# Up projections with 512 moving columns, first down projection in tokens, displaced activation slots, and 12 score bursts

## The chip, the cores and the metric

The kernel runs on one core of a Trainium2 chip. The engines of that core that matter are TensorE (PE: matmuls, and PEld: the load of a matmul's stationary operand), VectorE (DVE), ScalarE (ACT), GpSimd (POOL) and SyncE (SP, which issues most transfers). Each engine runs its own instructions strictly in the order in which they stand; semaphores tie the engines together. The metric is the device time of one execution in microseconds, as the median of several runs.

## The reference

A trunk of two layers over one sequence of 256 tokens with 1024 channels, all in float32:

```python
def hybrid_layer(x, ...):
    h = rmsnorm(x, norm_mix)
    proj = h @ w_in          # q, k, v of 24 heads of 64, and three gates of 1024
    ...                      # o_a: 12 dilated-window heads, o_b: 6 block heads, o_c: 6 stick-breaking heads
    merged = gates[:, :, 0] * (o_a @ w_out_a) + gates[:, :, 1] * (o_b @ w_out_b) + gates[:, :, 2] * (o_c @ w_out_c)
    x = x + merged @ w_o
    h = rmsnorm(x, norm_mlp)
    return x + jnp.square(jax.nn.relu(h @ w_up)) @ w_down     # 1024 -> 4096 -> 1024
# two layers, then one rmsnorm
```

The gates pass a sigmoid first. The dilated and block heads use a softmax; the stick-breaking heads use exponentials of sums of log-sigmoids.

## The kernel before

**Numbers.** Every value that TensorE multiplies is kept as two parts, `hi` (rounded to the type fp32r) and `lo` (the rest), and a product is the three matmuls lo·hi, hi·hi and hi·lo, added up in PSUM. ACT writes the `hi`, DVE the `lo`.

**Weights** come in 280 pieces of 128x1024 (`raw`), one transfer each, in the order of use. `split` makes `wh` (L118, ACT) and `wl` (L119, DVE) of a piece, three pieces ahead of TensorE, in 6 buffers each.

**Activations** lie with channels on the partitions: `xres` [128, 8, 256] is the residual. A normalised or scaled copy lies in one of two rotating slots `hl` [128, 2, 8, 256], first all `hi`, then all `lo`, written by `norm_split` (L158 ACT, L159 DVE). A `proj` (L198 to L200) takes one weight piece and 8 channel blocks: 24 matmuls with 256 moving columns.

**A layer, stage by stage.** (1) `v_chunk` (L243 to L245): V in tokens, with 512 moving columns. (2) `qk_pair` and `gate_tile`, in the order MIX_ORDER, and between them the attention units: `a0`, `a1` (six heads each, softmax), `b0` to `b2` (two heads each, softmax), `c0` to `c2` (two heads each, stick-breaking). A unit begins with a burst of score matmuls (`burst`, L283, 64 rows of contraction), then come ACT and DVE work on the scores, transposes (L377 to L379) and the PV matmuls (L310, L311); an `a` unit has two bursts, so that a layer has ten. After the last PV of a pair, `o_head` (ACT L297 `tmp`, DVE L298 `oF`) and `o_split` (ACT L301, DVE L302) write the head pair's channels into the slot `oT`. (3) The sigmoids of the eight gate tiles (L479), held back until after the last exponential, between two loads of the ACT tables (L479 and L482, the second in the first layer alone). (4) The merge: eight times a `proj` over `oT` into a two-bank PSUM tile `s` (two of them rotate), multiplied by the gates on DVE (L495), summed (L496, L497) and split (L498, L499). (5) `w_o`: eight `proj`, each added to `xres` (L507), then `norm_split`. (6) The MLP: `up_pair` makes two `proj` into one PSUM bank, then ACT Relu (L540), ACT Square (L542), DVE CAST (L545) and DVE subtract (L546). The down projection of the first layer, `down` (L557 to L559), has the weights stationary and 256 tokens moving, 768 matmuls; that of the last layer, `down_nat` (L583 to L585), has the activations stationary and 512 weight columns moving, 384 matmuls, with the result in tokens. The down projections of pair i-1 follow the ups of pair i; the last four pieces are kept for the end, where the result is finished part by part. For the first layer that end is: scale by R2 and add to `xres` on DVE (L644, L645), `norm_split`, next layer.

**Order.** The kernel is recorded in program order; a scheduler with priorities (for instance 400 for bursts, 300 for weight splits) then sets the order on each engine. An engine's order is fixed when the kernel is built.

## Time and profile before

| | us |
|---|---|
| median of three runs | 884.33 (883.89 to 885.01) |
| the profiled execution | 884.33 |
| its span, first to last instruction | 882.6 |
| PE busy | 870.9 (99%) |
| DVE busy | 598.9 (68%) |
| ACT busy | 494.2 (56%) |
| POOL busy | 50.7 (6%) |

The span is shorter than the time by 1.7 us that lie around it. The granted TensorE clock is 0.998 of full speed over the span, the higher of its two levels. "Busy" of an engine is the time in which at least one of its instructions was under way; matmuls overlap, so that a record of 0.28 us stands beside the next one 0.12 us later. What a matmul costs in a row of matmuls is therefore read from start to start.

### The profile page before, as it was taken

What the parts mean: (1) busy time and instruction counts of PE and PEld (TensorE: products, weight loads), DVE (VectorE), ACT (ScalarE), POOL (GpSimd) and SP (SyncE); (2) the same over time, 40 slices, a digit from 0 to 9 for tenths busy, and PEclk for the clock granted to TensorE, in tenths of its full rate; (3) what the DMA queues carried; (4) which work ended last, traced back from release to release, by engine and by line L of the source; (5) the groups of instructions that cost most, each with busy time, mean ns of one, the idle gap of its engine ahead of it and who ended that gap; (6) DMA issues with size and microseconds to landing.
All of it is one profiled execution on the core that took longest, in us unless ns stands there. A gap on an engine that the chain in (4) does not pass through costs nothing.

```text
span 882.6 us, 16351 instructions
## 1 busy us (share of the span) xinstructions
PE 870.9 (99%) x6648; PEld 833.1 (94%) x6648; DVE 598.9 (68%) x899; ACT 494.2 (56%) x732; POOL 50.7 (6%) x64
## 2 busy tenths in 40 slices
PE   8999999999999999999999999999999999999996
PEld 7899999999999999999988999999999999999995
DVE  6977878855886554555678878787567865555553
ACT  7756566758365444444466664666573554444442
POOL 3000101000030000000020101010000300000000
PEclk9999999999999999999999999999999999999999
DMA  9755443454556666666565554344554666666641
GB/s 316 258 173 159 144 143 121 155 160 151 180 181 186 187 187 181 180 188 184 151 196 187 174 162 142 122 141 146 168 167 145 214 192 191 189 190 187 189 127 48
DMA packets 43562, 151.47 MB, mean 172 GB/s; under 512 B 4960, under 2 KB 6368, under 8 KB 43488
## 3 DMA queue, kind: packets, MB, share of 16 engines
q1 hardware_dynamic: 43056, 149.90, 55.2%
q8 instruction: 52, 0.85, 0.4%
q10 hardware_dynamic: 432, 0.54, 0.2%
q14 instruction: 22, 0.18, 0.1%
HBM read 149.37 MB, written 1.05 MB: 170 GB/s over the span
## 4 chain that ended last, share of the span: by engine, by line
PE 94%; DVE 2%; DMA 1%; issue 1%; ACT 1%; SPq 0%; POOLq 0%; ACTq 0%
PE mm L198 18%; PE mm L199 18%; PE mm L200 18%; PE s L557 4%; PE s L559 4%; PE s L558 3%; PE s L583 3%; PE s L584 3%; PE s L585 3%; PE s L283 2%; PE s L198 2%; PE s L199 2%; PE s L200 2%; PE s L243 2%; PE s L245 2%; PE s L244 2%
## 5 line engine op out<-in xcount | busy, mean ns | idle before, releaser
L119 DVE TENSOR_TENSOR wl<-raw,wh 128x1024 fp32r<-128x1024 f32 (+1 forms) x282 | 343.8, 1222 | 221.7 <-ACT wh L118 221.1
L118 ACT ACTIVATE wh<-raw 128x1024 fp32r<-128x1024 f32 (+1 forms) x282 | 295.0, 1051 | 274.0 <-PE mm L200 151.1
L198 PE MATMUL mm<-hl,wl 128*128 128x256 f32 x1344 | 382.1, 285 | 1.9 <-DVE xres L507 1.9
L199 PE MATMUL mm<-hl,wh 128*128 128x256 f32 x1344 | 381.3, 284 | 0.0
L200 PE MATMUL mm<-hl,wh 128*128 128x256 f32 x1344 | 379.8, 284 | 0.0
L198 PEld LDWEIGHTS mm<-hl,wl 128*128 128x128 f32 x1344 | 257.3, 191 | 3.7 <-DVE xres L507 2.4
L199 PEld LDWEIGHTS mm<-hl,wh 128*128 128x128 f32 x1344 | 257.3, 192 | 0.9
L200 PEld LDWEIGHTS mm<-hl,wh 128*128 128x128 f32 x1344 | 256.7, 191 | 0.3 <-DVE hl L159 0.2
L557 PE MATMUL s<-ga,wl 128*128 128x256 f32 x256 | 72.6, 284 | 0.0
L558 PE MATMUL s<-ga,wh 128*128 128x256 f32 x256 | 72.4, 283 | 0.0
L559 PE MATMUL s<-ga,wh 128*128 128x256 f32 x256 | 72.2, 283 | 0.0
L169 POOL TENSOR_TENSOR acc<-acc,sq 128x256 f32<-128x256 f32 x28 | 26.9, 962 | 417.4 <-ACT sq L168 242.6
L583 PE MATMUL s<-wl,ga 128*128 128x512 f32 x128 | 50.1, 392 | 0.0
L584 PE MATMUL s<-wh,ga 128*128 128x512 f32 x128 | 50.0, 391 | 0.0
L557 PEld LDWEIGHTS s<-ga,wl 128*128 128x128 f32 x256 | 49.1, 192 | 0.4 <-DVE sq L644 0.2
L585 PE MATMUL s<-wh,ga 128*128 128x512 f32 x128 | 49.5, 389 | 0.0
L558 PEld LDWEIGHTS s<-ga,wh 128*128 128x128 f32 x256 | 49.1, 192 | 0.1
L559 PEld LDWEIGHTS s<-ga,wh 128*128 128x128 f32 x256 | 49.0, 192 | 0.2 <-DVE ga L546 0.2
L198 PE MATMUL s<-hl,wl 128*128 128x256 f32 x128 | 36.5, 285 | 0.0
L199 PE MATMUL s<-hl,wh 128*128 128x256 f32 x128 | 36.2, 283 | 0.0
L200 PE MATMUL s<-hl,wh 128*128 128x256 f32 x128 | 36.2, 283 | 0.0
L410 POOL TENSOR_SCALAR_AFFINE_SELECT wk<-wk 128x256 f32<-128x256 f32 x24 | 18.4, 790 | 221.2 <-DVE wk L422 152.2
(132 smaller groups left out, 1124.4 us busy)
## 6 DMA issues: line engine op xcount, KB each, us to landing
raw<-in_w_dram SPq DMA_DIRECT2D x278, 512.0 KB, 4.2
raw<-in_w_dram SPq DMA_DIRECT2D x4, 256.0 KB, 3.5
xres<-in_x_dram SPq DMA_DIRECT2D x8, 128.0 KB, 5.6
wk<-in_gfin_dram SPq DMA_DIRECT2D x2, 256.0 KB, 4.4
out_dram<-V SPq DMA_DIRECT2D x2, 256.0 KB, 2.3
out_dram<-V ACTq DMA_DIRECT2D x2, 256.0 KB, 2.1
c_maskA<-in_maskA_dram SPq DMA_DIRECT2D x1, 384.0 KB, 6.1
c_rope<-in_rope_dram SPq DMA_DIRECT2D x1, 256.0 KB, 5.7
```

The source lines that it names most:

```text
L118: act.activation(hi[:, c:c + step], r[:, c:c + step], AF.Copy)
L119: dve.tensor_tensor(lo[:, c:c + step], r[:, c:c + step], hi[:, c:c + step].bitcast(F32), op=ALU.subtract)
L169: pool.tensor_tensor(acc, acc, sq, op=ALU.add)
L198: pe.matmul(dst, lo[:, c:c + P], hl[:, 0, koff + k], start=a, stop=False, skip_group_check=True)
L199: pe.matmul(dst, hi[:, c:c + P], hl[:, 0, koff + k], start=False, stop=False, skip_group_check=True)
L200: pe.matmul(dst, hi[:, c:c + P], hl[:, 1, koff + k], start=False, stop=z, skip_group_check=True)
L557: pe.matmul(dst, lo[:, c], uh[:, j % 2], start=a, stop=False, skip_group_check=True)
L558: pe.matmul(dst, hi[:, c], uh[:, j % 2], start=False, stop=False, skip_group_check=True)
L559: pe.matmul(dst, hi[:, c], ul[:, j % 2], start=False, stop=z, skip_group_check=True)
L583: pe.matmul(dst, uh[:, j % 2, k], lo[:, c], start=j == 0, stop=False)
L584: pe.matmul(dst, uh[:, j % 2, k], hi[:, c], start=False, stop=False)
L585: pe.matmul(dst, ul[:, j % 2, k], hi[:, c], start=False, stop=j == 2 * npairs - 1)
```

## The change

**Wide up runs.** A new `proj_wide` takes a weight piece and moves `hi` and `lo` of a channel block as one run of 512 columns: 8 matmuls with `wh` stationary into the two halves of a bank, and 8 with `wl` stationary and 256 columns into the first half; 16 where 24 were. For that, `hi` and `lo` of a block lie side by side: the slots are [128, 8, 2, 256]. Each piece has a PSUM bank of its own. DVE adds the halves (`tensor_reduce`, over a strided view of the bank), for a pair of pieces DVE makes max(t,0)·t, ACT copies it into `uh`, DVE subtracts `ul`.

**First down in tokens.** Both layers use `down_nat`. At the end of the first layer's MLP each of four groups (128 tokens x 512 channels) is scaled on ACT, turned back by four transposes on PE, and added to `xres` on DVE; after the second token half of a channel half come four `norm_split`. The broadcast of R2 goes.

**Displaced slots.** The rotating slots `hl` become two fixed ones, `hl0` and `hl1`, and small unused tiles between `hl0`, `hl1`, `ga` and `wh` move the addresses of what follows them.

**Bursts of two units.** `together` sends the score matmuls of two units as one burst: per layer c0 with the first of a0, then the second of a0, c1 with the first of a1, the second of a1, c2 with b0, b1 with b2. Six per layer. A burst waits until all reads of the previous burst's banks that its units returned (a softmax's minimum pass, a `c` unit's last exponential) are done.

The diff, cut to its core (where only the index order of a slot changes, and where a unit only returns its jobs instead of sending them, lines are left out):

```diff
+
+
+    for tag, shape, bufs, dt in (("hl0", [P, KT, 2, S], 1, F32R),
+                                 ("skip0", [P, 24], 1, F32),
+                                 ("hl1", [P, KT, 2, S], 1, F32R),
+                                 ("skip1", [P, 56], 1, F32),
+                                 ("ga", [P, 3, S], KT, F32),
+                                 ("skip2", [P, 48], 1, F32),
+                                 ("wh", [P, 1024], W_BUFS, F32R), ("wl", [P, 1024], W_BUFS, F32R), ("V", [P, 2, 8, 2, DH], 3, F32R)):
+        T(tag, shape, bufs, dt)
...
-    def hilo_slot():
-        return T("hl", [P, 2, KT, S], 2, F32R)
+    def hilo_slot(i):
+        return T("hl%d" % i, [P, KT, 2, S], 1, F32R)
...
+    def proj_wide(n, hl, bank):
+
+        hi, lo = split(n)
+        for k in range(KT):
+            pe.matmul(bank, hi[:, k * P:k * P + P], hl[:, k].rearrange("p a b -> p (a b)"), start=k == 0, stop=False,
+                      skip_group_check=True)
+        for k in range(KT):
+            pe.matmul(bank[:, 0:S], lo[:, k * P:k * P + P], hl[:, k, 0], start=False, stop=k == KT - 1,
+                      skip_group_check=True)
 
     acc = T("acc", [P, S], 1)
-    hl = hilo_slot()
+    hl = hilo_slot(0)
     for d in range(KT):
         norm_split(hl, 0, d)
         sumsq(d, acc)
...
                 act.activation(t[:, 1], p3[:, 1], AF.Copy)
             QK[f] = t
 
-        def burst(jobs, after=None):
-
+        open_banks = []
+
+        def together(*units):
+
+            made = [u() for u in units]
             before = None
             with tc.high_priority(offset=BPRI):
-                for dst, f, j, qs, ks, flipped, first in jobs:
+                for dst, f, j, qs, ks, flipped, first in sum([m[0] for m in made], []):
                     t, own = QK[f], slice(j * DH, j * DH + DH)
                     q, k = t[own, 0, qs], t[own, 1, ks]
                     i = pe.matmul(dst, k if flipped else q, q if flipped else k, start=first, stop=True, skip_group_check=True)
-                    if before is None and after is not None:
-                        tc.add_manual_dep(i.ins, after.ins.name, READ, reason="the banks are free together")
-                    if before is not None:
+                    if before is None:
+                        for r in open_banks:
+                            tc.add_manual_dep(i.ins, r.ins.name, READ, reason="the banks are free together")
+                    else:
                         tc.add_manual_dep(i.ins, before.ins.name, QUEUED, reason="one burst of scores")
                     before = i
-
-        oT = hilo_slot()
+            open_banks.clear()
+            for m in made:
+                open_banks.append(m[1]())
+
+        oT = hilo_slot(0)
         last_exp = [None]
         T0, T1, TT = slice(0, P), slice(P, S), slice(0, S)
 
...
@@ -466,12 +503,19 @@
             {"v": v_chunk, "qk": qk_pair, "g": gate_tile}[kind](i, n)
             n += MIX_LEN[kind]
             group, u = ATT_AFTER.get((kind, i), (None, 0))
-            if group == "a":
-                att_softmax(QK_A[u], u, units)
+            if group == "c":
+                held.append(att_c(u))
+            elif group == "a" or (group == "b" and (held or u == 1)):
+                sc, va = att_softmax(QK_A[u], u) if group == "a" else att_softmax([QK_B[u]], 2 + u)
+                if group == "b" and not held:
+                    held.append((sc, va))
+                else:
+                    hs, hv = held.pop(0)
+                    units.append(lambda a=sc[0], b=hs[0]: together(a, b))
+                    units += [lambda a=a: together(a) for a in sc[1:]] + hv + va
             elif group == "b":
-                att_softmax([QK_B[u]], 2 + u, units)
-            elif group == "c":
-                att_c(u, units)
+                sc, va = att_softmax([QK_B[u]], 2 + u)
+                units += [lambda a=sc[0]: together(a)] + va
             run_units(UNIT_RATE[kind])
         run_units(len(units))
         with tc.issue_after(last_exp[0].ins):
...
-        if layer < DEPTH - 1:
-            R2 = T("tmp", [P, S], 2)
-            act.activation(R2, bcast(rcol), AF.Square)
 
...
         def up_pair(i):
-            p = mm_bank()
-            proj(p[:, 0:S], npc["u", 2 * i], hl)
-            proj(p[:, S:2 * S], npc["u", 2 * i + 1], hl)
-            s1 = T("wk", [P, 512], WK)
-            act.activation(s1, p, AF.Relu)
-            u = T("wk", [P, 512], WK)
-            act.activation(u, s1, AF.Square)
+            t = T("wk", [P, 2, S], WK)
+            for a in range(2):
+                p = mm_bank()
+                proj_wide(npc["u", 2 * i + a], hl, p)
+                dve.tensor_reduce(t[:, a], p.rearrange("p (a b) -> p b a", a=2), axis=mybir.AxisListType.X, op=ALU.add)
+            u = T("wk", [P, 2, S], WK)
+            dve.scalar_tensor_tensor(u, t, 0.0, t, op0=ALU.max, op1=ALU.mult)
             uh = T("ga", [P, 2, S], KT, F32R)
             ul = T("ga", [P, 2, S], KT, F32R)
-            dve.tensor_copy(uh.rearrange("p a b -> p (a b)"), u)
-            dve.tensor_tensor(ul.rearrange("p a b -> p (a b)"), u, uh.rearrange("p a b -> p (a b)").bitcast(F32), op=ALU.subtract)
+            act.activation(uh, u, AF.Copy)
+            dve.tensor_tensor(ul, u, uh.bitcast(F32), op=ALU.subtract)
             us[i] = (uh, ul)
-
-
-        def down(j, d):
...
-            r2 = T("rc", [P, 2], 8)
-            dve.tensor_tensor(r2, rcol, rcol, op=ALU.mult)
+        r2 = T("rc", [P, 2], 8)
+        dve.tensor_tensor(r2, rcol, rcol, op=ALU.mult)
 
         def down_nat(j, t, h):
             hi, lo = split(npc["d", j])
...
-        groups = [(t, h) for t in range(2) for h in range(2)] if last else [(d,) for d in range(KT)]
-        one = down_nat if last else down
+        groups = [(t, h) for t in range(2) for h in range(2)] if last else [(t, h) for h in range(2) for t in range(2)]
+        one = down_nat
         body = 2 * npairs - TAIL
         for i in range(npairs + 1):
             if i < npairs:
@@ -629,22 +655,27 @@
             finish(1)
             continue
         acc = T("acc", [P, S], 1)
-        hl = hilo_slot()
-        for d in range(KT):
-            if d == 0:
-                for e in range(SKEW):
-                    for j in range(body, 2 * npairs - 2):
-                        down(j, e)
-            if d + SKEW < KT:
+        hl = hilo_slot(0)
+        for i, (t, h) in enumerate(groups):
+            if i == 0:
                 for j in range(body, 2 * npairs - 2):
-                    down(j, d + SKEW)
+                    one(j, t, h)
+            if i + 1 < len(groups):
+                for j in range(body, 2 * npairs - 2):
+                    one(j, *groups[i + 1])
             for j in range(2 * npairs - 2, 2 * npairs):
-                down(j, d)
-            tmp = T("sq", [P, S], 3)
-            dve.tensor_tensor(tmp, down_dst(d), R2, op=ALU.mult)
-            dve.tensor_tensor(xres[:, d], xres[:, d], tmp, op=ALU.add)
-            norm_split(hl, 2 * layer + 2, d)
-            sumsq(d, acc)
+                one(j, t, h)
+            y = T("wk", [P, 512], WK)
+            act.activation(y, acc2[h][:, t], AF.Copy, scale=r2[:, t:t + 1])
+            tb = t_bank()
+            for d in range(4):
+                pe.transpose(tb[:, d * P:(d + 1) * P], y[:, d * P:(d + 1) * P], ident)
+            x4 = xres[:, 4 * h:4 * h + 4, t * P:(t + 1) * P]
+            dve.tensor_tensor(x4, x4, tb.rearrange("p (a b) -> p a b", a=4), op=ALU.add)
+            if t == 1:
+                for d in range(4 * h, 4 * h + 4):
+                    norm_split(hl, 2 * layer + 2, d)
```

What the change does to the order of instructions is shown at three places; all names are tiles with their numbers.

**The end of the attention of the first layer, PE.** `t_432` is the PSUM tile of the last head's PV, `s_460` the first tile of the merge, `mm_448` and `mm_455` the last gate tile's, `hl_23` is `oT`. Before, the last PV and the first of the merge:

```order
L311 MATMUL t_432_2403<-pl_435_2409,V_87_454 64x256
L310 MATMUL t_432_2403<-ph_434_2408,V_87_454 128x128
L311 MATMUL t_432_2403<-pl_435_2409,V_87_454 64x128
L198 MATMUL s_460_2619<-hl_23_169,wl_451_2519 128x256
L199 MATMUL s_460_2619<-hl_23_169,wh_450_2518 128x256
L200 MATMUL s_460_2619<-hl_23_169,wh_450_2518 128x256
```

Seven rows of `s_460` stand there, then 72 of the gates, and then the merge goes on:

```order
L198 MATMUL mm_455_2577<-hl_22_168,wl_447_2487 128x256
L199 MATMUL mm_455_2577<-hl_22_168,wh_446_2486 128x256
L200 MATMUL mm_455_2577<-hl_22_168,wh_446_2486 128x256
L199 MATMUL s_460_2619<-hl_23_169,wh_450_2518 128x256
L200 MATMUL s_460_2619<-hl_23_169,wh_450_2518 128x256
L198 MATMUL s_460_2619<-hl_23_169,wl_451_2519 128x256
```

Now (`t_441` is the last PV's tile, `s_469` and `s_474` the first two of the merge, `hl0_32` is `oT`):

```order
L336 MATMUL t_441_2412<-ph_443_2417,V_96_463 128x256
L337 MATMUL t_441_2412<-pl_444_2418,V_96_463 64x256
L336 MATMUL t_441_2412<-ph_443_2417,V_96_463 128x128
L337 MATMUL t_441_2412<-pl_444_2418,V_96_463 64x128
L207 MATMUL s_469_2628<-hl0_32_178,wl_460_2528 128x256
L208 MATMUL s_469_2628<-hl0_32_178,wh_459_2527 128x256
L207 MATMUL s_474_2665<-hl0_32_178,wl_463_2558 128x256
L208 MATMUL s_474_2665<-hl0_32_178,wh_462_2557 128x256
L209 MATMUL s_469_2628<-hl0_32_178,wh_459_2527 128x256
```

The gate matmuls now all stand ahead of the last PV, and so do 12 of the 24 matmuls of `s_469` and 12 of `s_474`; the next row reads the channel block that the last head pair fills.

**The same place, ACT.** Before (sigmoids of `ga`, weight splits `wh`):

```order
L297 ACTIVATE tmp_436_2416<-t_432_2403 64x256
L301 ACTIVATE hl_23_169<-oF_356_1990 128x256
L479 ACT_TABLE_LOAD
L479 ACTIVATE ga_24_170<-ga_24_170 128x768
L479 ACTIVATE ga_25_171<-ga_25_171 128x768
L479 ACTIVATE ga_26_172<-ga_26_172 128x768
L479 ACTIVATE ga_27_173<-ga_27_173 128x768
L479 ACTIVATE ga_28_174<-ga_28_174 128x768
L479 ACTIVATE ga_29_175<-ga_29_175 128x768
L479 ACTIVATE ga_30_176<-ga_30_176 128x768
L118 ACTIVATE wh_462_2622<-raw_461_2620 128x1024
L118 ACTIVATE wh_467_2659<-raw_466_2657 128x1024
```

Now:

```order
L327 ACTIVATE hl0_32_178<-oF_365_1999 128x256
L523 ACT_TABLE_LOAD
L523 ACTIVATE ga_33_179<-ga_33_179 128x768
L523 ACTIVATE ga_34_180<-ga_34_180 128x768
L523 ACTIVATE ga_35_181<-ga_35_181 128x768
L523 ACTIVATE ga_36_182<-ga_36_182 128x768
L523 ACTIVATE ga_37_183<-ga_37_183 128x768
L523 ACTIVATE ga_38_184<-ga_38_184 128x768
L523 ACTIVATE ga_39_185<-ga_39_185 128x768
L523 ACTIVATE ga_40_186<-ga_40_186 128x768
L526 ACT_TABLE_LOAD
L127 ACTIVATE wh_486_2742<-raw_485_2740 128x1024
```

All eight sigmoids and both table loads stand together, ahead of the first weight split. On DVE that split's other half, `wl_487`, stands ahead of the gate products (L539) from the fourth merge tile on:

```order
L539 TENSOR_TENSOR wk_483_2733<-s_479_2702,ga_35_181 128x768
L128 TENSOR_TENSOR wl_487_2743<-raw_485_2740,wh_486_2742 128x1024
L540 TENSOR_TENSOR wk_483_2733<-wk_483_2733 128x256
L128 TENSOR_TENSOR wl_492_2780<-raw_490_2777,wh_491_2779 128x1024
L543 TENSOR_TENSOR hl1_468_2627<-wk_473_2659,hl1_468_2627 128x256
L543 TENSOR_TENSOR hl1_468_2627<-wk_478_2696,hl1_468_2627 128x256
L541 TENSOR_TENSOR wk_483_2733<-wk_483_2733 128x256
L539 TENSOR_TENSOR wk_488_2770<-s_484_2739,ga_36_182 128x768
```

Ahead of the first of these rows stand the gate products of `s_469` and `s_474`, with their sums.

**From `w_o` into the MLP, PE, first layer.** `mm_536` and `mm_545` are the last tile of `w_o`, `mm_549` and `mm_557` the first of the ups. Before:

```order
L199 MATMUL mm_536_3174<-hl_459_2618,wh_523_3066 128x256
L200 MATMUL mm_536_3174<-hl_459_2618,wh_523_3066 128x256
L198 MATMUL mm_549_3227<-hl_501_2916,wl_529_3104 128x256
L199 MATMUL mm_549_3227<-hl_501_2916,wh_528_3103 128x256
L200 MATMUL mm_549_3227<-hl_501_2916,wh_528_3103 128x256
```

20 rows of `mm_549` and 20 of the next piece stand there ahead of the first that reads the seventh channel block. Now:

```order
L209 MATMUL mm_545_3183<-hl1_468_2627,wh_532_3075 128x256
L215 MATMUL mm_557_3232<-hl0_510_2925,wh_537_3112 128x512 x6
L215 MATMUL mm_561_3256<-hl0_510_2925,wh_542_3149 128x512 x6
L215 MATMUL mm_557_3232<-hl0_510_2925,wh_537_3112 128x512
L215 MATMUL mm_561_3256<-hl0_510_2925,wh_542_3149 128x512
L184 MATMUL t_550_3220<-ones_75,acc_509_2924 128x1 x2
L215 MATMUL mm_557_3232<-hl0_510_2925,wh_537_3112 128x512
L218 MATMUL mm_557_3232<-hl0_510_2925,wl_538_3113 128x256 x8
```

Twelve wide matmuls stand ahead of the first that reads the seventh block.

## Rows read from the trace of the kernel before

**Rows 1.** The page: busy time by engine; the chain that ended last, by engine.

```profile
PE 870.9 (99%) x6648; PEld 833.1 (94%) x6648; DVE 598.9 (68%) x899; ACT 494.2 (56%) x732; POOL 50.7 (6%) x64
...
PE 94%; DVE 2%; DMA 1%; issue 1%; ACT 1%; SPq 0%; POOLq 0%; ACTq 0%
```

**Rows 2.** The waits of PE, grouped: total us, times, longest us.

```profile
PE mm L198 <- DVE xres L507: 1.9, 2, 1.1
```

**Rows 3.** First attention, two stretches of MLP: us; busy PE, PEld, DVE, ACT, POOL.

```profile
53.42:202.00 148.58, 148.58 (x1260) 145.26 (x1261) 115.41 (x216) 91.77 (x157) 9.21 (x12) 1.00 0.49 150
264.00:430.00 166.00, 166.00 (x1384) 165.95 (x1384) 87.17 (x91) 79.27 (x90) 0.71 (x1) 1.00 0.63 185
719.07:831.27 112.20, 112.20 (x721) 102.62 (x721) 60.50 (x61) 54.12 (x62) 0.00 (x0) 1.00 0.64 192
```

**Rows 4.** Timeline of PE in the last layer's MLP: start us, duration us, instruction.

```profile
752.33 0.40 PE L583 MATMUL s<-wl,ga 128*128 128x512 f32 x1
...
754.85 0.39 PE L585 MATMUL s<-wh,ga 128*128 128x512 f32 x1
```

**Rows 5.** Timeline of PE around the first score burst.

```profile
53.02 0.28 PE L199 MATMUL mm<-hl,wh 128*128 128x256 f32 x1
53.14 0.28 PE L200 MATMUL mm<-hl,wh 128*128 128x256 f32 x1
53.35 0.93 PE L283 MATMUL s<-qk 64*128 64x256 f32 x8
54.20 0.39 PE L198 MATMUL mm<-hl,wl 128*128 128x256 f32 x1
54.42 0.28 PE L199 MATMUL mm<-hl,wh 128*128 128x256 f32 x1
```

**Rows 6.** Groups by line and shape: count, busy us, mean ns, idle before.

```profile
L119 DVE TENSOR_TENSOR wl<-raw,wh 128x1024 fp32r<-128x1024 f32 x278 | 340.7, 1229 | 216.4 <-ACT wh L118 215.9
L118 ACT ACTIVATE wh<-raw 128x1024 fp32r<-128x1024 f32 x278 | 292.6, 1057 | 272.4 <-PE mm L200 151.1 <-PE s L559 38.9 <-PE s L585 33.7
L557 PE MATMUL s<-ga,wl 128*128 128x256 f32 x256 | 72.6, 284 | 0.0
...
L546 DVE TENSOR_TENSOR ga<-wk,ga 128x512 fp32r<-128x512 f32 x32 | 22.2, 693 | 1.1
...
L495 DVE TENSOR_TENSOR wk<-s,ga 128x768 f32<-128x768 f32 x16 | 15.2, 952 | 1.3 <-PE s L200 1.3
L283 PE MATMUL s<-qk 64*128 64x256 f32 x96 | 14.7, 411 | 0.0
...
L268 DVE TENSOR_TENSOR qk<-mm,c_rope 128x512 f32<-128x512 f32 x18 | 12.1, 673 | 0.0
...
L283 PE MATMUL s<-qk 64*128 64x128 f32 x96 | 8.4, 280 | 0.0
```

**Rows 7.** The chain that ended last: start us, us, what it was.

```profile
245.24 0.51 DVE xres L507 x2
...
259.90 0.34 DVE xres L507
...
268.07 0.43 PE t L188 x2
...
702.48 0.44 PE t L572 x4
```

**Rows 8.** Timeline of ACT at the end of the first layer's attention.

```profile
202.56 0.38 ACT L297 ACTIVATE tmp<-t 64x256 f32<-64x256 f32 x1
204.00 0.42 ACT L301 ACTIVATE hl<-oF 128x256 fp32r<-128x256 f32 x1 [1.06 <-DVE oF L298]
204.44 1.28 ACT L479 ACT_TABLE_LOAD   x1
205.73 5.25 ACT L479 ACTIVATE ga<-ga 128x768 f32<-128x768 f32 x7
```

**Rows 9.** Timeline of PE at the same place: first gate row after the PV, first merge row after the gates.

```profile
202.12 0.28 PE L198 MATMUL mm<-hl,wl 128*128 128x256 f32 x1
...
210.76 0.28 PE L199 MATMUL s<-hl,wh 128*128 128x256 f32 x1
```

**Rows 10.** Timeline of DVE at the same place.

```profile
203.55 0.42 DVE L298 TENSOR_TENSOR oF<-t,tmp 64x256 f32<-64x256 f32 x1
...
211.96 2.36 DVE L119 TENSOR_TENSOR wl<-raw,wh 128x1024 fp32r<-128x1024 f32 x2 [7.08 <-ACT wh L118]
```

More of the change, by code (lines that the diff above doesn't have):

```diff
@@ L389, in values, with att_c @@
                     o_split(oF, kt_out)
-            units += [score] + [softmax_second] * (G == 3) + [lambda: values(0), lambda: values(1)]
-        def att_c(i, units):
+            return ([softmax_first, softmax_second] if G == 3 else [softmax_one]), [lambda: values(0), lambda: values(1)]
+        def att_c(i):
             f = QK_C[i]
@@ L414, in logs @@
                 st = s_bank()
-                burst([(st[:, j, 0:S], f, j, TT, T0, True, True) for j in range(2)]
-                      + [(st[:, j, S:384], f, j, T1, T1, True, False) for j in range(2)])
-                z = st[:, :, 0:384]
-                ab = T("wk", [P, 2, 384], WK)
-                act.activation(ab, z, AF.Abs)
-                act.activation(ab, ab, AF.Exp, scale=-1.0)
-                act.activation(ab, ab, AF.Ln, bias=1.0)
-                dve.scalar_tensor_tensor(ab, z, 0.0, ab, op0=ALU.max, op1=ALU.add)
@@ L423, in logs @@
-                strict(ab)
-                h, l = hl2(ab)
-                for j in range(2):
-                    for x in (h, l):
-                        pe.matmul(st[:, j, 0:384], negtri, x[:, j], start=False, stop=False, skip_group_check=True)
-                    for n, x in enumerate((h, l)):
-                        pe.matmul(st[:, j, P:S], negones, x[:, j, S:384], start=False, stop=n == 1, skip_group_check=True)
-                a = T("wk", [P, 2, 384], WK)
-                last_exp[0] = act.activation(a, z, AF.Exp)
@@ L432, in logs, with rest @@
-                strict(a)
-                env["a"] = hl2(a)
+                def rest():
+                    z = st[:, :, 0:384]
+                    ab = T("wk", [P, 2, 384], WK)
+                    act.activation(ab, z, AF.Abs)
+                    act.activation(ab, ab, AF.Exp, scale=-1.0)
+                    act.activation(ab, ab, AF.Ln, bias=1.0)
+                    dve.scalar_tensor_tensor(ab, z, 0.0, ab, op0=ALU.max, op1=ALU.add)
+                    strict(ab)
+                    h, l = hl2(ab)
+                    for j in range(2):
+                        for x in (h, l):
+                            pe.matmul(st[:, j, 0:384], negtri, x[:, j], start=False, stop=False, skip_group_check=True)
+                        for n, x in enumerate((h, l)):
+                            pe.matmul(st[:, j, P:S], negones, x[:, j, S:384], start=False, stop=n == 1, skip_group_check=True)
+                    a = T("wk", [P, 2, 384], WK)
+                    last_exp[0] = act.activation(a, z, AF.Exp)
+                    strict(a)
+                    env["a"] = hl2(a)
+                    return last_exp[0]
@@ L435, in values @@
+                return ([(st[:, j, 0:S], f, j, TT, T0, True, True) for j in range(2)]
+                        + [(st[:, j, S:384], f, j, T1, T1, True, False) for j in range(2)]), rest
             def values():
@@ L457, in trunk @@
         units = []
+        held = []
         def run_units(k):
```

99 lines of the change are left out of this document (45 added, 54 removed).

## The prediction

> **What bounds the kernel now.** I read the page first: PE is busy for 99% of the span, and the chain that ended last runs through PE for 94% of it [rows 1]. The grouped waits name only one repeated wait of PE, 1.9 us in two places [rows 2]. So the time is the PE stream plus a few stalls, and the change can act in two ways: it makes the stream shorter, or it makes PE wait where it did not. The second is the one to search for, because ACT and DVE hardly ever make PE wait now. The profiled execution took 884.33 us, which is also the median; 1.7 us of it lie around the span.
>
> **Price of a matmul.** Not the 284 ns of a record [rows 6], since records overlap, but start to start. In the first layer's MLP, 1384 matmuls of 256 columns took 166.00 us: 119.9 ns each [rows 3]. In the last layer ten iterations took 112.20 us and hold 480 such matmuls and 240 of 512 columns: (112.20 - 480 x 0.1199)/240 = 227.7 ns, the switches between the two forms included [rows 3]; inside a run, 11 spacings from 752.33 to 754.85, 2.52 us, give 229 ns [rows 4]. Doubling the columns thus adds 107.8 ns, and 12.1 ns of each matmul do not depend on columns.
>
> This is where a page speaks against the change: the Trainium skill, "TensorE: Matmul & The Clock Gate", section "Wait — 56ns, not 53.3ns?", gives a matmul N/2.4 ns plus about 2.5 ns. By it fewer, wider matmuls would hardly help: the two PE terms below would be about 1.3 and 1.0 us and not 6.3 and 4.7. The trace disagrees for this data type, with 12.1 ns, and decides.
>
> **The change part by part: what PE saves.**
> - Wide ups. A piece costs 24 x 119.9 = 2.878 us now and 8 x 227.7 + 8 x 119.9 = 2.781 after; 64 pieces: 6.2 us.
> - First down in tokens: 768 x 119.9 ns = 92.1 us against 384 x 227.7 = 87.4: 4.7 us.
> - Bursts. Around a burst the spacing before its first matmul is 0.21 instead of 0.12, the one after it 0.22 instead of 0.12: 0.19 us of switching at the edges [rows 5]. The eight matmuls themselves take 0.85 us, against 0.37 if the two row halves ran fully side by side (768 columns at 2.4 GHz and four times 12 ns), so up to 0.48 may be switching as well. I take 0.38 per burst, between 0.19 and 0.67. Twenty bursts (192 score matmuls [rows 6]) become twelve: 8 x 0.38 = 3.0 us, bounds 1.5 and 5.4.
> - The R2 broadcast goes: half of the pair that took 0.43 us in the chain [rows 7], 0.2 us. Sixteen fp32 transposes come: four of the same kind took 0.44 us [rows 7], so 1.8 us, and 0.2 for getting into and out of that type.
> Sum: 6.2 + 4.7 + 3.0 + 0.2 - 2.0 = 12.1 us shorter, bounds 9 and 14.5.
>
> **What PE will wait for.** The order of the changed kernel shows three places.
>
> (1) The end of the attention, both layers. Now 72 gate matmuls, 8.64 us from 202.12 to 210.76 [rows 9], lie between the last PV and the first merge matmul that needs the last heads. They hide the chain tmp 0.38, oF 0.42, hl 0.42, a table load of 1.28 and most of the sigmoids, 0.75 each [rows 8, 10]. In the changed order no gate matmul is left there; the next row of PE reads the last heads' channels. With time zero where `hl` is written: PE waits 1.5 us before it (0.38 + 0.42 + 0.42 and three handovers of about 0.1). Sigmoid 0 ends at 1.28 + 0.75 = 2.1, its product (0.95, L495 [rows 6]) at 3.1, where PE, 24 matmuls on, wants the bank at 2.9: 0.2. Then eight sigmoids end at 7.3 and the second table load at 8.6; `wh` takes 1.06, `wl` 1.2 [rows 6], so wl_487 ends at 10.9. Behind it on DVE stand 0.4 of sum, wl_492 (until about 12.4), three short passes, and only then the product that frees the bank of the fifth merge tile: about 14.4. PE wants that bank at 11.9: 2.5 us. First layer: 1.5 + 0.2 + 2.5 = 4.2. The last layer has no second table load; by the same steps the fifth tile's bank comes at 10.9 against 8.9 wanted, and the next weights 0.3 late: 1.5 + 0.2 + 2.3 = 4.0. Queued behind the late DVE passes are the `hl1` splits and the `w_o` weight splits, which PE needs only later. Together 8.2 us; I take off 0.5 for the chain's step through DVE at 245.24 [rows 7], which a later start will swallow: 7.7. Bounds: 3 (the head chain and half of the rest) and 10.
>
> (2) From `w_o` into the MLP, both layers. PE has 40 matmuls of 256 (4.8 us) as cover there now and still waits 1.9 us in all, for the chain of xres, hl and weight splits on DVE, whose last step is the 0.34 at 259.90 [rows 2, 7]. Twelve wide matmuls are 2.7 us of cover. 2.1 us less cover, of which the faster rest of the run takes up part, since the wide pieces' `wl` half needs no further `lo`: 0.75 more per layer, 1.5. Bounds 0 and 4.
>
> (3) The turn from layer one to two: each transposed group waits for its ACT copy (about 0.6) right behind its own last matmuls. Four such waits, partly filled with V matmuls: 1.5 against 0.7 to 1.1 of stalls now: 0.8. Bounds 0 and 2.5.
>
> Sum of new waits: 7.7 + 1.5 + 0.8 = 10.0 us.
>
> Costed at nothing. The evictions in the MLP: a strided reduce has no row; the nearest are a plain 512 pass from PSUM at 0.67 and one at 0.69 [rows 6]. Per iteration of about 11 us DVE then has four `wl` of 1.2, two reduces and two passes, some 7.5 us; the cover is PE's 11 us, and it would fail only with reduces of over 2.4 us. Of PSUM the Trainium skill ("Advanced Engine Details and Errata", section "Memory Cachelines") says that every two consecutive elements should be contiguous; no run here shows that yet, and it alone would not reach PE. ACT loses two passes per pair and gains one. The displaced slots: matmuls of now show no spacing other than 119.9 over 1384 of them [rows 3]; I take zero, with 3 ns per matmul either way as a bound for the some 2700 that read `hl1`, 8 us. The wait of a burst for the previous one's reads: behind it PE's whole queue stands still, and who waits for that is every projection; my steps through the first burst (c0 with a0) give 10.0 us of ACT, DVE and POOL work until its next PE step against 10.3 us of PE work there, so nothing, but narrowly.
>
> **Sum.** 884.33 - 12.1 + 10.0 = 882.2 us. The gain is nearly given back.
>
> **The rivals.**
> - *The cover holds.* If ACT and DVE are less late at the end of the attention (PE itself being later there, by the chains before it), only the head chain of 1.5 us per layer stays, and with (2) and (3): 884.3 - 12.1 + 5.3 = 877.5. For it: PE in the trace nearly never waits for ACT and DVE. Against it: the order is fixed, and no gate matmul is left to fill. Displaced slots that save 3 ns would land lower still, at 870 to 875. Together 0.24.
> - *Longer attention chains, slower.* A c unit's scores now share burst, ACT and DVE with an a unit's. Decisive point: the 10.3 us of PE work up to the first triangle matmul of a c unit; each further microsecond of chain is a stall, six times in the kernel. With 1.2 us more each: 882.2 + 7.2 = 889.4; with half of it 886. For it: the margin of 0.3 us, and ACT and DVE are busy for 62% and 78% of the attention [rows 3]. Against it: PE now passes ten bursts per layer with no wait at all. Chance 0.26.
> - *Even.* Switching saves only the edges (1.5 in place of 3.0) and the new waits are as reckoned: 883.7; or new waits of 12 us: 884.2. Chance 0.16 beyond what the forecast's own spread holds.
> - *The change does not do what it says:* if a 512 wide run that is half `hi`, half `lo` cost more than the 227.7 of the last layer's downs, the ups would save nothing: 888. Nothing in the trace speaks for it; counted with the slower case.
>
> **How the numbers follow.** The forecast, 880 to 884.4 with 882.2 in the middle, has 0.34, of which some 0.26 lies below 882.56, which is 0.2% under the time of now (a measurement of this kernel can tell about that much from no change). Faster: 0.24 + 0.26 = 0.50. Within 0.2% (882.6 to 886.1): 0.08 of the forecast and 0.16 of the even case: 0.24. Slower: 0.26. The range leaves out 0.1 at each end: low end 873.0, where the rival of the held cover and a little of the slots lie, high end 889.0, nearly the full price of the longer chains. The forecast's own range is 880 to 884.4.
>
> **What would show it.** Right: in the MLP of both layers an iteration step of about 11.0 us in the chain (11.52 and 11.22 now); spacings of 0.12 and 0.227 in the ups; a PE stall of about 1.5 us right after the last PV and one of about 2 us at the fifth merge tile, released by DVE, in both layers; twelve bursts. Wrong: no PE wait at the merge (then the first rival), PE waits at L427's successor or at the bursts of 1 us or more (then the second), an up piece of over 2.85 us (then the last), or spacings of 256 columns that differ from 119.9 ns between the slots.

## The result and the profile after

The changed kernel takes 890.95 us (890.35 to 892.57) against 884.52 us of the kernel before: a ratio of 1.0076, 95% interval 1.0059 to 1.0093. It is slower, and lies outside the forecast range of 873.0 to 889.0. The profiled execution has a span of 889.0 us against 882.6.

The page of the changed kernel, the lines that answer to [rows 1]:

```profile
PE 868.9 (98%) x5766; PEld 788.3 (89%) x5766; DVE 642.4 (72%) x950; ACT 475.0 (53%) x703; POOL 43.0 (5%) x64
...
PE 88%; DVE 5%; ACT 3%; issue 2%; DMA 1%; SPq 0%; POOLq 0%; ACTq 0%; DVEq 0%
```

PE is busy for only 2.0 us less, not 12.1, and the chain that ended last now runs through DVE and ACT for 8%. The waits of PE, grouped (total us, times, longest us), in the place of [rows 2]:

```profile
PE s L207 <- ACT hl L327: 2.9, 2, 1.4
PE s L207 <- DVE wk L539: 2.6, 2, 2.2
PE mm L215 <- DVE xres L551: 1.9, 2, 1.0
PE mm L215 <- DVE hl L168: 1.7, 2, 0.9
```

The first two stand at the end of the attention, the other two at the start of the MLP. The times of the stages, read from the starts of PE's rows at their borders (first projection after V, first up matmul, first down matmul of the last four pieces, first q projection of the second layer):

| stage | before | after | difference | forecast |
|---|---|---|---|---|
| first layer, q to `w_o` | 214.92 | 218.65 | +3.7 | +2.4 |
| first layer, MLP up to the last four pieces | 174.98 | 171.95 | -3.0 | -6.4 |
| turn to the second layer, with its V | 45.87 | 47.85 | +2.0 | +2.0 |
| second layer, q to `w_o` | 214.93 | 218.18 | +3.3 | +2.3 |
| second layer, MLP up to the last four pieces | 172.09 | 172.44 | +0.4 | -2.4 |
| start and end together | | | +0.1 | 0 |

Only the turn came out as forecast. The attention stages miss by 2.3 us together, the MLP stages by 6.2.

**End of the attention.** Timeline of PE in the changed kernel, first layer, in the place of [rows 9]:

```profile
212.19 0.22 PE L337 MATMUL t<-pl,V 128*64 128x128 f32 x1
213.85 0.39 PE L207 MATMUL s<-hl,wl 128*128 128x256 f32 x1 [1.43 <-ACT hl L327]
...
225.62 0.28 PE L209 MATMUL s<-hl,wh 128*128 128x256 f32 x1
228.12 0.38 PE L207 MATMUL s<-hl,wl 128*128 128x256 f32 x1 [2.23 <-DVE wk L539]
```

The timeline of ACT at the same place, in the place of [rows 8]:

```profile
213.38 0.42 ACT L327 ACTIVATE hl<-oF 128x256 fp32r<-128x256 f32 x1 [0.48 <-DVE oF L324]
213.81 1.28 ACT L523 ACT_TABLE_LOAD   x1
215.11 5.98 ACT L523 ACTIVATE ga<-ga 128x768 f32<-128x768 f32 x8
221.11 1.28 ACT L526 ACT_TABLE_LOAD   x1
222.40 2.01 ACT L127 ACTIVATE wh<-raw 128x1024 fp32r<-128x1024 f32 x2
```

PE stops for 1.43 us right after the last PV and for 2.23 us at the fifth merge tile, 14.3 us after `hl`'s end at 213.80; the forecast had 1.5 and 2.5 us, and 14.4.

**Start of the MLP.** The chain of the changed kernel there:

```profile
263.50 0.34 DVE xres L551
...
263.88 3.69 PE mm L215 x8
```

The stretch by engines (the granted clock is the number behind the five busy times; 1.00 is 2.4 GHz):

```profile
264.00:268.00 4.00, 4.00 (x13) 3.27 (x14) 2.28 (x4) 0.68 (x2) 1.13 (x1) 0.58 0.79 223
```

Eight wide matmuls take 3.69 us here, 0.46 each: the clock is at 1.2 GHz for most of this stretch. PE had waited twice just before, 0.82 us behind its row at 260.29 and 0.97 behind the one at 262.42. The second layer has the same two waits, and there the granted clock stays at 1.00.

**Iterations of the MLP.** The chain of the changed kernel (first matmuls of an iteration's first up piece):

```profile
303.93 1.83 PE mm L215 x8
...
315.10 1.82 PE mm L215 x8
```

An iteration (two up pieces and their 24 downs) takes 11.17 us, in both layers, where 11.03 would follow from the forecast's prices. The ups cost what was forecast (1.83 us for eight wide matmuls and 0.95 for eight of 256 columns); the downs do not. Their spacing, from the timeline of PE in the second layer, in the place of [rows 4]:

```profile
736.63 0.40 PE L609 MATMUL s<-wl,ga 128*128 128x512 f32 x1
...
739.90 0.39 PE L611 MATMUL s<-wh,ga 128*128 128x512 f32 x1
```

14 spacings in 3.27 us are 233.6 ns, where [rows 4] gave 229 and a whole run of 24 in the kernel before gives 227.9.

### The profile page after: what moved, and what is told of

Read it like the earlier page. It is cut to its first block, busy times and chain, and to the rows that moved or that the text cites. A ratio compares the mean times of both kernels' runs of the same rounds, so it can differ in the third digit from the quotient of the medians.

```text
span 889.0 us, 14658 instructions
## 1 busy us (share of the span) xinstructions
PE 868.9 (98%) x5766; PEld 788.3 (89%) x5766; DVE 642.4 (72%) x950; ACT 475.0 (53%) x703; POOL 43.0 (5%) x64
## 4 chain that ended last, share of the span: by engine, by line
PE 88%; DVE 5%; ACT 3%; issue 2%; DMA 1%; SPq 0%; POOLq 0%; ACTq 0%; DVEq 0%
PE mm L215 13%; PE mm L207 10%; PE mm L208 10%; PE mm L209 10%; PE mm L218 7%; PE s L609 7%; PE s L611 7%; PE s L610 7%; DVE wl L128 2%; PE s L305 2%; PE s L262 2%; PE s L264 2%; PE s L263 2%; ACT ga L523 1%; PE s L207 1%
## 5 line engine op out<-in xcount | busy, mean ns | idle before, releaser
L207 PE MATMUL mm<-hl,wl 128*128 128x256 f32 x832 | 236.5, 285 | 0.5 <-ACT ga L491 0.5
L208 PE MATMUL mm<-hl,wh 128*128 128x256 f32 x832 | 235.4, 283 | 0.0
L209 PE MATMUL mm<-hl,wh 128*128 128x256 f32 x832 | 234.6, 283 | 0.0
L207 PEld LDWEIGHTS mm<-hl,wl 128*128 128x128 f32 x832 | 156.6, 188 | 1.5 <-ACT ga L491 0.9
L208 PEld LDWEIGHTS mm<-hl,wh 128*128 128x128 f32 x832 | 156.8, 189 | 1.0 <-issue 0.7
L209 PEld LDWEIGHTS mm<-hl,wh 128*128 128x128 f32 x832 | 156.6, 189 | 0.7 <-issue 0.7
L215 PE MATMUL mm<-hl,wh 128*128 128x512 f32 x512 | 131.3, 396 | 3.6 <-DVE xres L551 1.9
L215 PEld LDWEIGHTS mm<-hl,wh 128*128 128x128 f32 x512 | 94.9, 190 | 23.9 <-DVE xres L551 2.6
L609 PE MATMUL s<-wl,ga 128*128 128x512 f32 x256 | 101.6, 397 | 0.0
L610 PE MATMUL s<-wh,ga 128*128 128x512 f32 x256 | 101.2, 395 | 0.0
L611 PE MATMUL s<-wh,ga 128*128 128x512 f32 x256 | 100.6, 395 | 0.0
L218 PEld LDWEIGHTS mm<-hl,wl 128*128 128x128 f32 x512 | 69.9, 190 | 4.9
L578 DVE TENSOR_REDUCE wk<-mm 128x256 f32<-128x512 f32 x64 | 44.2, 691 | 40.0 <-PE mm L218 39.8
L218 PE MATMUL mm<-hl,wl 128*128 128x256 f32 x512 | 71.5, 282 | 0.0
L611 PEld LDWEIGHTS s<-wh,ga 128*128 128x128 f32 x256 | 48.0, 188 | 11.6
L609 PEld LDWEIGHTS s<-wl,ga 128*128 128x128 f32 x256 | 48.2, 188 | 10.6 <-DVE V L644 0.3
L610 PEld LDWEIGHTS s<-wh,ga 128*128 128x128 f32 x256 | 48.1, 188 | 10.1
```

Of the source, the lines that this page charges most:

```text
L207: pe.matmul(dst, lo[:, c:c + P], hl[:, koff + k, 0], start=a, stop=False, skip_group_check=True)
L208: pe.matmul(dst, hi[:, c:c + P], hl[:, koff + k, 0], start=False, stop=False, skip_group_check=True)
L209: pe.matmul(dst, hi[:, c:c + P], hl[:, koff + k, 1], start=False, stop=z, skip_group_check=True)
L215: pe.matmul(bank, hi[:, k * P:k * P + P], hl[:, k].rearrange("p a b -> p (a b)"), start=k == 0, stop=False, skip_group_check=True)
L218: pe.matmul(bank[:, 0:S], lo[:, k * P:k * P + P], hl[:, k, 0], start=False, stop=k == KT - 1, skip_group_check=True)
L578: dve.tensor_reduce(t[:, a], p.rearrange("p (a b) -> p b a", a=2), axis=mybir.AxisListType.X, op=ALU.add)
```

## The experiments

All times are medians, with the lowest and the highest run. The kernel before, run beside each group, had medians of 884.3 to 884.5 us.

**Without the small tiles (e1).** The changed kernel with

```diff
-                                 ("skip0", [P, 24], 1, F32),
-                                 ("skip1", [P, 56], 1, F32),
-                                 ("skip2", [P, 48], 1, F32),
```

> The changed kernel without the three small unused tiles, so that the slots, the up results and the weights lie as far from a 256 byte line as before. Theory A (the displaced addresses made the 512 column down matmuls slower): their spacing goes from 233 ns back to 228 ns in both layers, 768 times 5.5 ns = 4.2 us less, about 886.7 us, all other stages as in the changed kernel. Rival B (the downs are slower because of the new evictions beside them, the strided reduces on DVE): spacing stays at 233 ns and the time at 891 us.

Measured: 886.48 us (884.37 to 887.90). The timeline of PE in the second layer:

```profile
736.24 0.40 PE L606 MATMUL s<-wl,ga 128*128 128x512 f32 x1
...
739.65 0.39 PE L606 MATMUL s<-wl,ga 128*128 128x512 f32 x1
```

The chain in the first layer (first matmuls of two successive iterations):

```profile
304.11 1.81 PE mm L212 x8
...
315.14 1.81 PE mm L212 x8
```

15 spacings in 3.41 us: 227.3 ns; an iteration takes 11.03 us, in both layers. Theory A holds, B falls: the evictions are the same.

**The up results back to their offset (e6).** As the changed kernel, with

```diff
-                                 ("skip1", [P, 56], 1, F32),
+                                 ("skip1", [P, 40], 1, F32),
-                                 ("skip2", [P, 48], 1, F32),
```

> The changed kernel with only the up results (and what follows them) moved back to the offset they had before; the second activation slot keeps its displaced address. Theory A with the up results as the cause: downs at 228 ns, about 886.7 us, as without any small tile. If the second slot's address matters instead (it is read by q, k, gates and w_o, not by the downs), the downs stay at 233 ns and 891 us stands. The projections from the second slot should stay at 120 ns in either case.

Measured: 886.14 us (885.18 to 888.53). The first and the last of 24 downs in the second layer:

```profile
733.97 0.40 PE L608 MATMUL s<-wl,ga 128*128 128x512 f32 x1
...
739.21 0.39 PE L610 MATMUL s<-wh,ga 128*128 128x512 f32 x1
```

23 spacings in 5.24 us: 227.8 ns. Up to the next up piece 24 downs take 5.468 us, as in e1 (5.467), against 5.605 in the changed kernel. So it is the place of `ga`, which holds `uh` and `ul`, the stationary side of the downs. The second slot's address does nothing: matmuls that read it keep 120 ns here and in the changed kernel.

**Two other offsets of the up results (e10, e11).** On e3 below, `ga` lies 128 (e10) and 32 (e11) bytes off the weights' offset in a line of 256. The small tiles against those of the changed kernel, e10 first:

```diff
-                                 ("skip0", [P, 24], 1, F32),
-                                 ("skip1", [P, 56], 1, F32),
+                                 ("skip1", [P, 32], 1, F32),
-                                 ("skip2", [P, 48], 1, F32),
+                                 ("skip2", [P, 32], 1, F32),
```

```diff
-                                 ("skip0", [P, 24], 1, F32),
-                                 ("skip1", [P, 56], 1, F32),
+                                 ("skip1", [P, 8], 1, F32),
-                                 ("skip2", [P, 48], 1, F32),
+                                 ("skip2", [P, 56], 1, F32),
```

> 20 bursts, wide ups, token-major first down; the up results 128 bytes off the weights' offset in a 256 byte line (64 bytes off gave 233 ns per down matmul, no displacement 227 ns). If any offset of the stationary data against the moving data costs, 233 ns or more; if only offsets that are no multiple of 128 bytes cost, 227 ns.

> The same with the up results 32 bytes off the weights' offset. If any displacement costs alike, 233 ns per down matmul; if the cost goes with the distance, between 227 and 233; if 32 bytes do not matter, 227 ns.

Measured, one run each: 882.34 and 883.61 us, against 879.45 for e3. Timeline of PE of e10:

```profile
739.58 0.39 PE L601 MATMUL s<-wl,ga 128*128 128x512 f32 x1
...
742.83 0.39 PE L603 MATMUL s<-wh,ga 128*128 128x512 f32 x1
```

And of e11:

```profile
740.88 0.40 PE L601 MATMUL s<-wl,ga 128*128 128x512 f32 x1
...
743.90 0.40 PE L602 MATMUL s<-wh,ga 128*128 128x512 f32 x1
```

14 spacings in 3.25 us and 13 in 3.02: 232 ns both; 24 downs take 5.58 and 5.59 us. All three displaced offsets tried (32, 64, 128 bytes) cost about alike. Why, no run shows. Nor does one part the distance between `ga` and the weights from the place of `ga` by itself: the weights moved only by whole multiples of 256 bytes.

**Narrow ups (e4).** The changed kernel with `up_pair` as it was before the change:

```diff
-            for a in range(2):
-                p = mm_bank()
-                proj_wide(npc["u", 2 * i + a], hl, p)
...
+            p = mm_bank()
+            proj(p[:, 0:S], npc["u", 2 * i], hl)
+            proj(p[:, S:2 * S], npc["u", 2 * i + 1], hl)
+            s1 = T("wk", [P, 512], WK)
+            act.activation(s1, p, AF.Relu)
...
```

> The changed kernel with the narrow ups of before (24 matmuls of 256 columns, Relu, Square, cast), all else as changed. Theory A: downs stay at 233 ns, an up piece costs 2.88 us instead of 2.79 (64 x 0.09 = 5.8 us more), and the wait between w_o and the first ups shrinks from 3.7 and 2.6 us to about 1.3 each (3.6 us less): about 893 us. Rival B: the downs return to 228 ns as well (4.2 us less): about 889 us. If the clock's fall at the start of the MLP hangs on that wait, it goes too.

Measured: 891.66 us (891.05 to 892.27). 24 downs take 5.60 us, an iteration 11.34: theory A again, since neither wide ups nor strided reduces are left. The wait for `xres` at the start of the MLP is 1.6 us in two places and the one for `hl` is gone; the granted clock is 1.00 there.

**Every unit its own burst (e2).** The changed kernel with 20 bursts:

```diff
-                    units.append(lambda a=sc[0], b=hs[0]: together(a, b))
...
+                units += [lambda a=a, f=not m: together(a, fresh=f) for m, a in enumerate(sc)] + va
...
+            if fresh:
+                open_banks.clear()
```

> The changed kernel with every attention unit's scores in a burst of their own again (20 bursts). Theory C (the joined bursts move the gate matmuls ahead of the last PV and so uncover the chain at the end of the attention): gate matmuls lie again between the last PV and the merge, the stalls there (4.9 us in the first layer, 4.6 in the second) go, the eight further bursts cost 2.6 us, so about 884.0 us. Rival D (the stalls come from the wide slots' layout, the fixed slots or the weight splits' order, not from the joining): the stalls stay and the bursts come on top, about 893.5 us.

Measured: 882.94 us (882.53 to 885.54), 8.0 us less than the changed kernel: theory C, D falls. 72 gate matmuls lie behind the last PV again; the last PV, the first gate row and the last in the first layer:

```profile
201.70 0.22 PE L339 MATMUL t<-pl,V 128*64 128x128 f32 x1
...
202.64 0.28 PE L207 MATMUL mm<-hl,wl 128*128 128x256 f32 x1
...
211.16 0.29 PE L209 MATMUL mm<-hl,wh 128*128 128x256 f32 x1
```

The longest waits of PE that are left:

```profile
PE mm L215 <- DVE xres L544: 1.9, 2, 1.0
PE mm L215 <- DVE hl L168: 1.6, 2, 0.8
```

Both waits at the merge are gone, and the attention stages are back at 215.04 and 214.98 us (from 218.65 and 218.18): 6.8 us less in the profiled executions. Part of the 8.0 hangs on the clock. Seven of the ten runs show a mean granted clock of 0.998 and took 882.5 to 883.3 us; three show 0.994 to 0.996 and took 884.6 to 885.5, the profiled one among them, where the clock falls at the start of both MLPs. The four runs of the changed kernel all show 0.994 to 0.996.

The edit undoes two things at once: the joining, and the wait of a burst for the reads of the burst before it, which the change brought in with it. e13 below joins without that wait ahead of its joined bursts; no run has the wait alone.

**Only b1 and b2 apart (e7).** The changed kernel with b1 and b2 each in a burst of its own, 14 in all:

```diff
-            elif group == "a" or (group == "b" and (held or u == 1)):
+            elif group == "a" or (group == "b" and held):
...
-                if group == "b" and not held:
-                    held.append((sc, va))
```

> The changed kernel with only the last joined burst of each layer (b1 with b2) taken apart: 14 bursts. Theory C1 (that burst alone delays the end of the attention, since b1 must wait for b2's q and k): the gate matmuls lie behind the last PV again, the two stalls of 4.9 and 4.6 us go but for 0.5 each, two bursts cost 0.7, about 883 us. Theory C2 (every joined burst delays the chain a little): the stalls shrink only in part, 886 to 889 us.

Measured: 887.28 us (885.49 to 888.94). The waits of PE:

```profile
PE s L207 <- ACT hl L327: 2.9, 2, 1.4
...
PE s L207 <- DVE wk L536: 0.5, 1, 0.5
```

The wait at the fifth tile is nearly gone, the one behind the last PV stays: still no gate matmul stands behind it. That is C2: the earlier joins use the gates up too.

**Both undone (e3).** The edits of e1 and e2 together.

> The changed kernel with 20 bursts again and without the small unused tiles; wide ups and the token-major first down stay. If the two causes are independent, their savings add up: 8.0 us (bursts) and 4.6 us (addresses) off 891.0, so about 878.4 us, 0.7% under the kernel before. If they overlap (one stall hides the other), about 882 us.

Measured: 879.45 us (879.05 to 879.65), ratio to before 0.9944 (0.9929 to 0.9958). The two causes add up within about 1 us.

**The first pair of ups narrow (e8).** e3 with, in `up_pair`,

```diff
+            if i < 1:
+                p = mm_bank()
+                proj(p[:, 0:S], npc["u", 2 * i], hl)
+                proj(p[:, S:2 * S], npc["u", 2 * i + 1], hl)
...
+            else:
...
+                    proj_wide(npc["u", 2 * i + a], hl, p)
```

> As with 20 bursts and without small tiles, and the first pair of ups of each layer narrow as before (48 matmuls of 256 columns as cover). Theory E (the wide start costs cover): the waits at the start of the MLP go from 3.7 and 2.6 us to about 1.3 each, the clock stays up there, the two narrow pairs cost 2 x 0.2 us: 3 us less than with the wide start, about 875.5 us. Rival F (the wait is set by DVE and ACT, whatever PE does ahead of it): the wait only moves, 878.4 us.

Measured: 877.27 us (876.80 to 878.00), ratio to before 0.992 (0.9905 to 0.9935). The waits of PE for the residual:

```profile
PE mm L212 <- DVE xres L541: 1.6, 2, 0.8
```

The wait for `hl` (1.6 us in e3, in two places) is gone, and the one for `xres` is 1.6 instead of 1.9: theory E, at 2.2 us instead of 3. The clock has a part in it. The start of the second MLP in e3, then in e8:

```profile
692.00:696.00 4.00, 4.00 (x14) 3.33 (x15) 2.36 (x4) 0.65 (x2) 1.12 (x1) 0.57 0.77 238
692.00:696.00 4.00, 4.00 (x33) 3.78 (x31) 2.79 (x6) 1.06 (x1) 1.68 (x2) 1.00 0.76 253
```

At 0.57 over 4 us, e3 loses 1.7 us of work there; e8 loses none. Waits and clock together would give 3.6 us, less 0.4 for the two narrow pairs; what takes back 1 us of that, no run isolates. This is the fastest of all kernels here.

**The first down in channels (e9).** e3 with the first layer's `down`, R2 and last pieces as before the change:

```diff
-        one = down_nat
+        one = down_nat if last else down
...
+            R2 = T("tmp", [P, S], 2)
+            act.activation(R2, bcast(rcol), AF.Square)
...
```

> As with 20 bursts and without small tiles, but the first layer's down projection with the weights stationary and 256 tokens moving, as before (768 matmuls, R2, no transposes). By the rows the token-major form saves 0.37 us per pair of pieces in 14 iterations (5.0 us), and loses about 2 us at the turn to the next layer: this kernel then takes about 3 us more, 881.4 us. If the turn costs all of it, 878.4 us.

Measured: 882.57 us (881.43 to 884.20), 3.1 us more than e3. The chain in the first layer:

```profile
303.81 1.84 PE mm L212 x8
...
315.16 1.84 PE mm L212 x8
```

An iteration takes 11.35 us, against 11.03 with downs in tokens.

**Narrow ups on e3 (e12).** e3 with `up_pair` as before the change, the edit of e4.

> 20 bursts, no small tiles, token-major first down, and narrow ups as before. The wide ups cost 2.79 us a piece against 2.88 by the traces, 64 x 0.09 = 5.8 us; less the waits that the wide start costs (about 3 us): this kernel should take 3 us more than with wide ups and a wide start (879.45), about 882.3, and 5.4 us more than with a narrow first pair only (877.27). If the wide ups' evictions on DVE cost elsewhere, the difference is smaller.

Measured: 881.81 us (881.26 to 882.85): 2.4 us more than e3, and 4.5 more than e8. The wide ups pay, and nearly half of their gain needs the narrow start.

**Only the early joins (e13).** e8 with c0 and a0, c1 and a1 in shared bursts, 16 in all:

```diff
+            if group == "c" and u < 2:
+                held.append(att_c(u))
+            elif group == "a":
+                sc, va = att_softmax(QK_A[u], u)
+                hs, hv = held.pop(0)
+                units.append(lambda a=sc[0], b=hs[0]: together(a, b, fresh=True))
...
```

> 20 bursts less the two that c0 shares with a0 and c1 with a1 in each layer (8 per layer), narrow first pair, no small tiles. If early joins are free of the late chain: four bursts fewer at 0.2 to 0.3 us each, 876.3 us. If every join delays the attention's end (the b1, b2 experiment points that way), gates are again used up early and the wait of 1.4 us per layer returns: 879 us or more.

Measured: 880.63 us (880.28 to 880.71), 3.4 us more than e8. The waits of PE:

```profile
PE s L204 <- ACT hl L326: 1.7, 2, 0.9
...
PE s L204 <- DVE wk L535: 0.5, 1, 0.5
```

No gate matmul is left behind the last PV here either, though the late units are apart. Nor did these joins save burst time: on PE the eight score matmuls of the last unit fall into two runs, of six and two (at 167.42 and 168.58 in the first layer), and a layer's bursts take 9.86 us, against 9.85 in e8.

## Why the prediction was wrong

The sum was 884.3 - 12.1 + 10.0 = 882.2; the kernel took 8.8 us more. The savings of PE came as forecast; the term put at nothing and two of the three waits did not.

**Right.** The price of a wide piece: without the small tiles an iteration of the second layer's MLP goes from 11.22 to 11.03 us, 0.19 x 32 iterations = 6.1 us of 6.2 forecast (the 6.3 beside the page's price is the same term). By an estimate from the rule weighed ahead (the Trainium skill, "TensorE: Matmul & The Clock Gate", section "Wait — 56ns, not 53.3ns?") it would have been about 0.04 us per iteration; the runs stand against it for these matmuls. The downs in tokens: 11.35 to 11.03, 0.32 x 16 = 5.1 against 4.7. The turn: +2.0 as forecast, though 0.25 of it is the displaced tiles (47.85 us, 47.60 in e1), so that the form itself cost a little less. The bursts: six take 9.1 us in the first layer where ten took 9.8, and four pairs of edges at 0.19 go: 1.5 per layer, 3.0 as forecast. The strided reduce costs 691 ns, as much as the plain passes it was priced by [rows 6], and no wait of PE is put down to it:

```profile
L578 DVE TENSOR_REDUCE wk<-mm 128x256 f32<-128x512 f32 x64 | 44.2, 691 | 40.0 <-PE mm L218 39.8
```

**Wrong, first: the displaced slots, taken at zero.** The step looked at the wrong tiles. It bounded what reads `hl1`, from a row with no displaced address in it; what mattered was `ga`, the stationary side of 768 downs. 768 x 5.7 ns (5.605 against 5.467 us for 24) = 4.4 us, of which 3.8 lie in the MLP stages; e1 and e6 gave back 4.5 and 4.8 us. The bound of 8 us either way would have covered it, but only its faster side was given a chance.

**Wrong, second: the start of the MLP, forecast at 1.5 us.** The waits there rose by 1.7 (1.9 to 1.9 and 1.7), close to the forecast. Behind them the clock fell in the first layer: granted 0.58 over 4 us, that is 1.7 us of work at full speed lost, in a stage where every matmul is on the path. The forecast had no term for the clock at all. 1.9 us missed; with the 3.8 of the slots that is 5.7 of the 6.2 by which the MLP stages miss, and 0.5 stay open.

**Wrong, third: the end of the attention, forecast at 7.7 us of new waits and about 10 measured** (7.0 of the two stages and the 3.0 that the bursts save). The two waits were sized well in the first layer. In the second the bank wait is short by the trace (2.6 in both layers, of which 2.2 in the first), but the clock fell there as well:

```profile
650.00:654.00 4.00, 2.49 (x14) 2.18 (x15) 1.23 (x3) 2.50 (x4) 0.00 (x0) 0.88 0.40 133
654.00:658.00 4.00, 4.00 (x27) 4.00 (x26) 2.73 (x4) 4.00 (x7) 0.00 (x0) 0.69 0.01 4
```

0.5 + 1.2 us of work lost: PE arrives later, and so waits less, 0.33 us for the bank. The credit of 0.5 was wrong: the 0.44 us step before the fifth `w_o` tile stands in both layers as before. (It is a second repeated wait, 0.3 us in two places, beside the one that the prediction read as the only one.) So the two waits (2.9 and 2.6) and the clock (1.7) make 7.2 of the 10 us. Of the other 2.8, smaller steps up to the last PV make 1.8: in each layer one of 0.50 us, at 148.79 in the first, and two of 0.38 and 0.37, at 211.59 and 211.96, where 0.12 is usual. No run isolates them.

Why no gates are left for the end can be read from the trace. A joined burst starts only when both units' q and k are there: the first burst of the layer starts at 71.25 us, before the change at 53.35 [rows 5]. ACT has less to do in between; before and after (the fourth busy time is ACT's):

```profile
53.00:71.00 18.00, 18.00 (x150) 17.70 (x149) 16.20 (x24) 11.01 (x13) 2.44 (x4) 1.00 0.59 178
53.00:71.00 18.00, 18.00 (x152) 18.00 (x151) 15.50 (x22) 6.72 (x7) 0.00 (x0) 1.00 0.65 205
```

PE goes on with projections meanwhile (18.00 of the 18 us in both), and the last PV comes at 212.19 instead of 201.18. That the late start alone sets this end is argued, not shown.

**The rivals.** The slower one named longer chains in the attention that would stall PE six times. That did not happen: PE passes the first five bursts' chains with one step of 0.50 us in each layer. The late end of the attention, which the forecast had in its own sum, is what the joining costs: e2 undoes it and gains 8.0 us (6.8 in the attention stages of the profiled execution), the bursts' own saving already lost again. The two early joins alone (e13) move the gates ahead, and the last one on top of the others (e7) costs 3.7 us more; the join of c2 with b0 was not tried by itself.

## What to carry to other kernels

Before instructions are merged to save switching, ask what work they will leave over for the place where a chain ends: here 3 us of switching saved cost about 10 us at the end of the attention, 1.7 of them by the clock. Ask too whether work that is ready early would then wait for a partner that is ready late. A stage that starts behind a long chain wants its cheapest-to-wait form first (many small matmuls over few inputs), and the efficient form from the second step on. An address is a part of a change: move tiles in an experiment of their own and read the spacing of every matmul that touches them, on the stationary side too.

## What the runs showed of the hardware

The offset of the stationary operand's tile: at 32, 64 and 128 bytes from the weights' offset within 256 bytes a 512 column fp32r matmul took 232 to 234 ns, at the same offset 227 to 228. Matmuls that move 256 columns out of a displaced slot (`hl1`, 96 bytes) kept 120 ns; a displaced stationary tile with 256 columns is in no run. What in the chip makes the difference, no run here shows.

The clock: in the kernel before it is granted at 1.00 in every stretch after the start until the end; in the profiled execution of the changed kernel it falls to 1.2 GHz twice, behind a wait of 1.4 us or two of 1.0 and 0.8 close together. The waits alone do not settle it: the same ones stand in both layers of that execution, and each kind is followed by a fall in one layer only. In the profiled execution of e7 it does not fall although those waits are there; in e1 it falls in the merge of the first layer and at the start of the second MLP.

The same kernel can take either course from run to run. In e2, e7 and e9 the longer runs are those with a lower mean granted clock (e7: 885.7 us at 0.998, 888.4 and 888.9 at 0.994; e9: 881.4 to 881.9 at 0.999, 883.6 and 884.2 at 0.994); in e1 and e6 the two do not go together, and what else scatters there no run shows. e8, where of these waits only 0.8 us at the start of each MLP is left, shows 0.998 or 0.999 in all four runs.
